# The FFN's second projection by tokens, in seven block products set between the slabs of the first projection

## The chip, the core and the metric

The kernel runs on one core of a Trainium2 chip. The metric is the device time of one launch in microseconds (us), taken over repeated runs. A core has five engines that run their own instruction streams and wait for one another by semaphores: TensorE (PE in the profile, with its weight loads as PEld), VectorE (DVE), ScalarE (ACT), GpSimd (POOL) and SyncE (SP), which here only issues DMA transfers. Matmul results land in PSUM, which has eight buffers of 128 x 512 float32 in this kernel (four in the pool mm, four in ms); everything else lies in SBUF.

## The reference

One step of a one-layer decoder: a mixer (a gated MLP and a state-space branch) and then the FFN that the change touches. There are 256 prompt tokens and 64 sample tokens (8 sequences of 8), D = 2048 and an inner width of 5632 in two halves, g and u.

```python
def conv_ffn(h, conv_state, w_up, conv_w, conv_b, w_down):
    up = h @ w_up
    up, new_conv = causal_depthwise_conv(up, conv_state, conv_w, conv_b)
    g, u = jnp.split(up, 2, axis=-1)
    return (jax.nn.gelu(g, approximate=True) * u) @ w_down, new_conv

def rms_norm(x, w):
    xf = x.astype(jnp.float32)
    y = xf * lax.rsqrt(jnp.mean(xf * xf, axis=-1, keepdims=True) + EPS)
    return (y * w.astype(jnp.float32)).astype(x.dtype)

f, new_ffn_conv = conv_ffn(rms_norm(x, p["norm_ffn_pre"]), ffn_conv_state, ...)
x = x + rms_norm(f, p["norm_ffn_post"])
```

All inputs and outputs are float32. `h @ w_up` is the first projection (2048 to 11264), `... @ w_down` the second (5632 to 2048).

## The kernel before, in words

**Precision.** A product of two float32 matrices is made of three matmuls on rounded parts: each operand is split into a high part (rounded to the type float32r, by ScalarE) and a low part (what is left, by VectorE), and high x high, low x high and high x low are added up (`accumulate`, L131; its three matmuls are lines L134 to L136). A matmul on plain float32 operands is recorded as two passes.

**Layout.** Activations are kept with features on partitions and the 320 tokens along the free axis. Weights are the stationary operand, 128 x 128, and tokens move, 320 columns.

**Slabs.** Weights come in slabs of 512 KB (`slab`, L109): SP loads the raw slab (tile wraw), ScalarE rounds it (whi, L123), VectorE takes the difference (wlo, L124). Each of the three tiles has three buffers. The block is marked with `tc.high_priority(offset=100000)`; `first()` (L103) is a stronger mark. The Tile planner fixes the order of each engine's queue when the kernel is built: it goes by these priorities and by its own costs, and an engine then takes its instructions strictly in that order.

**First projection.** `project` (L175) handles 512 output features, 4 PSUM buffers of the pool mm: 8 slabs of 512 KB, each with 24 matmuls, and after each slab it calls `tick()` (L157), which lets a background task from the list `bg` advance by one step (up to its next `yield`). In the FFN no background task is left. `ffn_up(g)` calls it twice (half 0: the columns of g, half 1: those of u) for the 512 features of chunk g; there are 11 chunks. `evac(half, j, ps)` takes one block of 128 features out of PSUM: VectorE scales it into tile pad (L1329, L1330), ScalarE and VectorE do the convolution (L1336, L1338), ScalarE the gelu; for half 1 VectorE multiplies the halves (L1347, L1348) and `split` makes the parts fhi and flo (L396, L397). GpSimd does small copies (L1326, L1327, L1340, L1341).

**Second projection.** `chunk_out(w, ck, hi, lo, ...)` (L234) multiplies one chunk's 4 x 128 features by 512 rows of w_down: 16 output blocks of 128, each 12 matmuls with 320 columns, after which the block is added to the tile acc_ffn (L247; chunk 0 copies it on ScalarE). The loop at L1409 first makes `ffn_up(g + 1)` and then `chunk_out` of chunk g, so that the gate of chunk g + 1 runs while PE works on chunk g. In the chunk before the last, VectorE turns x (tile x1_tok) into token order meanwhile (L1404).

**Last norm.** While the last chunk runs, each finished block is squared, scaled by the gain and turned to tokens in 32 x 32 blocks; then PE sums the squares over partitions (L1426, L1429), the root is taken on 10 columns (L1433 to L1438), and the scaled f and x are added by VectorE (L1474) and, for three of ten token groups, by ScalarE and PE (L1452, L1454, L1459). The output y is stored in a turned layout that the host puts right.

## Time and profile before

| what | value |
|---|---|
| time, median of 3 runs | 1748.42 us (1748.28 to 1748.61) |
| span of the profiled execution, first to last instruction | 1746.8 us |
| granted TensorE clock, mean over the span | 1.000 |
| one steady chunk (1000.5 to 1085.0 us): second projection of one, first projection of the next | 28.2 + 56.3 us |
| VectorE busy in these | 22.85 + 28.52 us |
| last matmul of the last chunk starts | 1732.62 us |

The page gives no other time of the profiled execution than its span; around the span the runs show 1.6 us more (1748.42 - 1746.8). In group lines the columns are line, engine, operation, out<-in, shape and count, and behind the bar busy us, mean ns of one, and the idle time ahead of it with what ended it. In the windows each engine has its busy time and its number of instructions.

### The profile page before, as it was taken

What the parts mean: (1) busy time and instruction counts of PE and PEld (TensorE: products, weight loads), DVE (VectorE), ACT (ScalarE), POOL (GpSimd) and SP (SyncE); (2) the same over time, 40 slices, a digit from 0 to 9 for tenths busy, and PEclk for the clock granted to TensorE, in tenths of its full rate; (3) what the DMA queues carried; (4) which work ended last, traced back from release to release, by engine and by line L of the source; (5) the groups of instructions that cost most, each with busy time, mean ns of one, the idle gap of its engine ahead of it and who ended that gap; (6) DMA issues with size and microseconds to landing.
All of it is one profiled execution on the core that took longest, in us unless ns stands there. A gap on an engine that the chain in (4) does not pass through costs nothing.

```text
span 1746.8 us, 31126 instructions
## 1 busy us (share of the span) xinstructions
PE 1738.5 (100%) x12063; PEld 1719.3 (98%) x12063; DVE 1178.0 (67%) x2009; ACT 819.4 (47%) x1198; POOL 323.5 (19%) x684
## 2 busy tenths in 40 slices
PE   9999999999999999999999999999999999999998
PEld 9999999999999999999999999999999999999997
DVE  6549863657879787778954566565756565657587
ACT  6344545334656664646544434343434343333336
POOL 2432230000423323121210101020201010101002
PEclk9999999999999999999999999999999999999999
DMA  8786655456676777665655554545544545454543
GB/s 257 230 231 183 183 176 154 151 163 192 214 221 208 218 225 210 211 187 155 195 154 151 151 154 149 150 155 147 159 145 151 155 149 152 152 153 151 148 158 109
DMA packets 228803, 303.85 MB, mean 174 GB/s; under 512 B 21680, under 2 KB 152624, under 8 KB 228464
## 3 DMA queue, kind: packets, MB, share of 16 engines
q1 hardware_dynamic: 211264, 272.68, 51.7%
q0 software_dynamic: 6176, 13.87, 2.7%
q10 hardware_dynamic: 11216, 15.31, 2.6%
q8 instruction: 95, 1.56, 0.4%
q14 instruction: 52, 0.43, 0.1%
HBM read 280.80 MB, written 19.69 MB: 172 GB/s over the span
## 4 chain that ended last, share of the span: by engine, by line
PE 99%; DMA 0%; ACT 0%; DVE 0%; SPq 0%; issue 0%; ACTq 0%
PE ps L134 21%; PE ps L135 20%; PE ps L136 20%; PE pd L134 10%; PE pd L135 10%; PE pd L136 10%; PE y_ps L1086 1%; PE ps_v L134 1%; PE ps_v L136 1%; PE ps_v L135 1%; PE yo_ps L1001 0%; PE up_ps L1018 0%; PE sg L808 0%; DMA wraw<-in_w_in 0%; PE fin_ps L1167 0%; PE xt_ps L412 0%
## 5 line engine op out<-in xcount | busy, mean ns | idle before, releaser
L124 DVE TENSOR_TENSOR wlo<-wraw,whi 128x1024 fp32r<-128x1024 f32 (+2 forms) x480 | 584.7, 1219 | 420.6 <-ACT whi L123 417.8
L123 ACT CAST whi<-wraw 128x1024 fp32r<-128x1024 f32 (+2 forms) x479 | 495.4, 1034 | 693.4 <-PE ps L135 392.3
L134 PE MATMUL ps<-h_hi,whi 128*128 128x320 f32 x2428 | 752.2, 310 | 0.0
L135 PE MATMUL ps<-h_lo,whi 128*128 128x320 f32 x2428 | 750.6, 309 | 0.0
L136 PE MATMUL ps<-h_hi,wlo 128*128 128x320 f32 x2428 | 750.0, 309 | 0.0
L134 PEld LDWEIGHTS ps<-h_hi,whi 128*128 128x128 f32 x2428 | 455.7, 188 | 3.1 <-issue 1.3
L135 PEld LDWEIGHTS ps<-h_lo,whi 128*128 128x128 f32 x2428 | 455.9, 188 | 0.4
L136 PEld LDWEIGHTS ps<-h_hi,wlo 128*128 128x128 f32 x2428 | 455.7, 188 | 0.0
L134 PE MATMUL pd<-fhi,whi 128*128 128x320 f32 x704 | 217.4, 309 | 0.0
L135 PE MATMUL pd<-flo,whi 128*128 128x320 f32 x704 | 217.4, 309 | 0.0
L136 PE MATMUL pd<-fhi,wlo 128*128 128x320 f32 x704 | 217.4, 309 | 0.0
L134 PE MATMUL pd<-ohi,whi 128*128 128x320 f32 x448 | 138.7, 310 | 0.0
L136 PE MATMUL pd<-ohi,wlo 128*128 128x320 f32 x448 | 138.3, 309 | 0.0
L135 PE MATMUL pd<-olo,whi 128*128 128x320 f32 x448 | 138.3, 309 | 0.0
L1341 POOL COPY ptf<-pad 128x2 f32<-128x2 f32 x88 | 22.0, 250 | 601.4 <-DVE pad L1329 600.8
L136 PEld LDWEIGHTS pd<-fhi,wlo 128*128 128x128 f32 x704 | 132.4, 188 | 0.0
L134 PEld LDWEIGHTS pd<-fhi,whi 128*128 128x128 f32 x704 | 132.3, 188 | 0.0
L135 PEld LDWEIGHTS pd<-flo,whi 128*128 128x128 f32 x704 | 132.3, 188 | 0.0
L247 DVE TENSOR_TENSOR acc_ffn<-acc_ffn,pd 128x320 f32<-128x320 f32 (+1 forms) x161 | 77.2, 480 | 29.8 <-PE pd L136 28.2
L134 PEld LDWEIGHTS pd<-ohi,whi 128*128 128x128 f32 x448 | 84.1, 188 | 0.6
L135 PEld LDWEIGHTS pd<-olo,whi 128*128 128x128 f32 x448 | 84.1, 188 | 0.3
L136 PEld LDWEIGHTS pd<-ohi,wlo 128*128 128x128 f32 x448 | 84.1, 188 | 0.0
(353 smaller groups left out, 1725.0 us busy)
## 6 DMA issues: line engine op xcount, KB each, us to landing
wraw<-in_ffn_w_up SPq DMA_DIRECT2D x176, 512.0 KB, 3.7
wraw<-in_w_in SPq DMA_DIRECT2D x132, 512.0 KB, 3.8
wraw<-in_ffn_w_down SPq DMA_DIRECT2D x88, 512.0 KB, 3.4
wraw<-in_w_out SPq DMA_DIRECT2D x64, 512.0 KB, 3.5
st<-in_state_ssm SPq DMA_DIRECT2D x40, 256.0 KB, 4.6
out_ssm_state_sample<-st ACTq DMA_DIRECT2D x30, 256.0 KB, 2.3
cs<-dacs_d SPq DMA_DIRECT2D x16, 320.0 KB, 5.3
wraw<-in_w_in SPq DMA_DIRECT2D x12, 384.0 KB, 3.8
```

The source lines that it names most:

```text
L123: rounded[:] = [act.copy(hi, raw).ins]
L124: lowered[:] = [dve.tensor_tensor(out=lo, in0=raw, in1=hi.bitcast(F32), op=ALU.subtract).ins]
L134: pe.matmul(ps, whi, xhi, start=first, stop=False)
L135: pe.matmul(ps, whi, xlo, start=False, stop=False)
L136: last_made[0] = pe.matmul(ps, wlo, xhi, start=False, stop=last).ins
L247: added_last[:] = [dve.tensor_tensor(out=acc[:, nb, ts], in0=acc[:, nb, ts], in1=ps[:, ts], op=ALU.add).ins]
L1086: pe.matmul(ps[64 * i:64 * i + 64, cols], w(hl), x(hl, m, cpx), tile_position=(0, 64 * i), **flags)
L1341: pool.tensor_copy(ptf[:, k, :], pad[:, 256:258])
```

## The change

The second projection is turned round: tokens become the stationary operand (128 at a time) and 512 columns of w_down move. The result has tokens on partitions.

For the 256 prompt tokens a chunk's product is cut into blocks: the activations into 2 x 2 (128 tokens by 256 features, names a11 to a22), and for each half m of the output columns (1024 of 2048) the weights into 2 x 2 (256 features by 512 columns, b11 to b22). Strassen's scheme in Winograd's form makes seven block products of these, with sums s1 to s4 on the activations' side and t1 to t4 on the weights' side. Each product is 6 matmuls. The seven products are summed over the chunks each for itself (tiles in_mix and in_fp); `together(m)` combines them once, at the end. The 64 sample tokens are multiplied in plain float32, two groups of 512 columns beside each other in the array by `tile_position`.

The second projection of chunk g - 1 is now a background task (`down_steps`) of `ffn_up(g)`: after each slab of the first projection one step, that is one product, is issued; the first two steps are empty and 14 follow. Chunks 0 to 9 go this way; the last has no first projection left beside it and is done in eight plain products (`down_plain`). The weight sums t1 to t4 are made by GpSimd, t2 to t4 in place in the loaded blocks. x is turned into token order after `ffn_up(0)` and written to DRAM (x1_rows), and read back at the end. The last norm works on rows of tokens, block by block (`one_block`, `whole`). The host turns the columns of w_down and the gain beforehand and the result afterwards.

```diff
-    def slab(src, half=0, begins=False):
+    def slab(src, half=0, begins=False, kept=None):
...
+            raw, hi, lo = (t[:, m * half:m * half + m] for t in (both[:1] + list(kept) if kept else both))
...
-            hi = fp.tile([P, 4, NT], F32R, tag="fhi", name="fhi", bufs=2)
-            lo = fp.tile([P, 4, NT], F32R, tag="flo", name="flo", bufs=2)
+            a = hp.tile([P, 4, NP], F32, tag="ohi", name="a")
+            a_s = fp.tile([P, 4, NS], F32, tag="a_s", name="a_s", bufs=2)
+            parts = Parts(a, a_s, g == NG - 1)
...
-                split(hi[:, j, :], lo[:, j, :], a)
+                parts.there(j)
...
+        class Parts:
...
+            def cut(self, name):
+                self.hi[name] = fp.tile([P, 2, P], F32R, name=f"{name}_hi")
+                self.lo[name] = fp.tile([P, 2, P], F32R, name=f"{name}_lo")
+                split(self.hi[name], self.lo[name], self.block(name))
+
+            def there(self, j):
...
+                if j == 1:
+                    self.cut("a11")
+                    if self.plain:
+                        self.cut("a21")
+                    else:
+                        combined("s3", "a11", ALU.subtract, "a21")
+                        self.cut("s3")
+                elif j == 3:
+                    self.cut("a12")
+                    self.cut("a22")
+                    if not self.plain:
+                        combined("s1", "a21", ALU.add, "a22")
+                        combined("s2", "s1", ALU.subtract, "a11")
+                        combined("s4", "a12", ALU.subtract, "s2")
+                        for name in ("s1", "s2", "s4"):
+                            self.cut(name)
+
         nxt = ffn_up(0)
-        for g in range(NG):
-            hi, lo = nxt
-            if g < NG - 1:
-                nxt = ffn_up(g + 1)
...
-            chunk_out(ffn_w_down, g, hi, lo, g == 0, done, apart=g == NG - 1)
+        for i in range(4):
+            st = hp.tile([P, SN, 4, 32], F32, tag=("ohi", "olo")[i % 2], name="in_turn")
+            dve.transpose(out=st, in_=x1[:, 4 * i:4 * i + 4].rearrange("p k (s f) -> p s k f", f=32))
+            for q in range(4):
+                e = 512 * q + P * i
+                pool.dma_start(x1_rows[:, e:e + P].rearrange("(s t) e -> t s e", t=32), st[32 * q:32 * q + 32].rearrange("p s k f -> p s (k f)"))
+
+        in_mix = hp.tile([P, 9, 512], F32, tag="acc_mix", name="in_mix")
...
+        def taken_in(to, ps, begins):
+            with first():
+                if begins:
+                    act.copy(to, ps)
+                else:
+                    dve.tensor_tensor(out=to, in0=to, in1=ps, op=ALU.add)
...
+        def sample_products(ps, a_s, k0, w, start, stop):
+            for k in range(2):
+                for h in range(2):
+                    last_made[0] = pe.matmul(ps[64 * h:64 * h + 64], a_s[:, k0 + k], w[h][:, 512 * k:512 * k + 512], start=start and k == 0,
+                                             stop=stop and k == 1, tile_position=(0, 64 * h)).ins
+
+        def down_steps(ck, parts):
+            def ready(raw):
+                with tc.high_priority(offset=100000):
+                    hi, lo = (wp.tile([P, 1024], F32R, tag=t, name=t, bufs=3) for t in ("whi", "wlo"))
+                    act.copy(hi, raw)
+                    dve.tensor_tensor(out=lo, in0=raw, in1=hi.bitcast(F32), op=ALU.subtract)
+                return hi, lo
+            yield
+            yield
+            for m in range(2):
...
+                def less(to, x, y):
+                    with tc.high_priority(offset=100000):
+                        pool.tensor_tensor(out=to, in0=raw[x], in1=raw[y], op=ALU.subtract)
...
+                for name in ("b11", "b12", "b22", "b21"):
+                    load(name)
+                product(1, "a11", "b11")
+                yield
+                raw["t1"] = fp.tile([P, 1024], F32, name="t1")
+                less(raw["t1"], "b12", "b11")
+                ps = misc("pms")
+                sample_products(ps, parts.a_s, 0, (raw["b11"], raw["b12"]), True, False)
+                sample_products(ps, parts.a_s, 2, (raw["b21"], raw["b22"]), False, True)
+                taken_in(f_s[m], ps, ck == 0)
+                product(2, "a12", "b21")
+                yield
+                raw["t3"] = raw["b12"]
+                less(raw["t3"], "b22", "b12")
+                product(5, "s1", "t1")
+                yield
+                raw["t2"] = raw["b11"]
+                less(raw["t2"], "b22", "t1")
+                product(7, "s3", "t3")
+                yield
+                raw["t4"] = raw["b21"]
+                less(raw["t4"], "t2", "b21")
+                product(3, "s4", "b22")
+                yield
+                product(6, "s2", "t2")
+                yield
+                product(4, "a22", "t4")
+                yield
...
+        for g in range(1, NG):
+            steps = down_steps(g - 1, nxt)
+            bg.append(steps)
+            nxt = ffn_up(g)
+            while bg:
+                advance(bg, steps)
+        for m in range(2):
+            together(m)
...
+        def one_block(c, nb):
+            t, g, _ = of(c, nb)
+            ends = c == 0 and nb == 3
+            with first() if ends else nullcontext():
+                act.activation(unread, t, AF.Square, accum_out=squares[:, c, nb:nb + 1])
+                (dve if ends else pool).tensor_tensor(out=t, in0=t, in1=g, op=ALU.mult)
+            if nb == (1 if c == 2 else 3):
+                whole(c)
...
+                for nb in range(2 if c == 2 else 4):
+                    t, _, y = of(c, nb)
+                    if nb == 2:
+                        act.activation(unread, t, AF.Copy, scale=r)
+                        pool.tensor_tensor(out=y, in0=unread, in1=y, op=ALU.add)
+                    else:
+                        dve.scalar_tensor_tensor(out=y, in0=t, scalar=r, in1=y, op0=ALU.mult, op1=ALU.add)
...
+        act.activation(fp.tile([P, 1], F32, name="root_ready"), eps, AF.Sqrt)
+        down_plain(NG - 1, nxt, one_block)
```

`down_plain` takes w_down in slabs as `chunk_out` did, multiplies each by the blocks of both token groups, 96 matmuls with 512 columns in all, and does the samples as above. In its second half the products of the first token group come last, from weights that are kept until then.

More of the change, by code (lines that the diff above doesn't have):

```diff
@@ L1382, in ffn_up @@
                 act.dma_start(o_fconv_s[:, k:k + 4], stg[:, half])
[L1383 to L1385 removed]
+            return parts
         eps = fp.tile([P, 1], F32, name="eps")
         pool.memset(eps, EPS)
[L1388 to L1400 removed]
@@ L1420, in hybrid_step @@
-        act.dma_start(o_fconv_p, ptf)
-        ps = misc("tsum")
-        with tc.issue_after(pd_last[-1]):
-            made = pe.matmul(ps[:, :NT], ones, sq4, start=True, stop=False).ins
-        for ts in parts_of(KD - 1):
-            with tc.issue_after(made):
-                made = pe.matmul(ps[:, ts], ones, one[0][:, ts], start=False, stop=ts.stop == NT).ins
-        sums = fp.tile([P, SN, 32], F32, name="sums")
-        dve.transpose(out=sums, in_=ps[:, :NT].rearrange("p (s f) -> p s f", f=32))
```

197 lines of the change are left out of this document (128 added, 69 removed).

## The prediction

> **What bounds the kernel now.** I read the page first (the span, busy shares, the chain that ended last, the groups), then the windows of one steady chunk of the FFN, then the chain in order of time for the cost of single products, then forms, waits and timelines.
>
> ```profile
> span 1746.8 us, 31126 instructions
> PE 1738.5 (100%) x12063; PEld 1719.3 (98%) x12063; DVE 1178.0 (67%) x2009; ACT 819.4 (47%) x1198; POOL 323.5 (19%) x684
> PE 99%; DMA 0%; ACT 0%; DVE 0%; SPq 0%; issue 0%; ACTq 0%
> ```
> ```profile
> 1000.50:1028.70 28.20, 28.20 (x195) 28.20 (x194) 22.85 (x43) 10.98 (x14) 3.58 (x10) 1.00 0.50 152
> 1028.70:1085.00 56.30, 56.30 (x386) 56.30 (x386) 28.52 (x42) 22.11 (x26) 6.69 (x23) 1.00 0.50 152
> ```
> ```profile
> 1000.49:1028.66 28.17, 28.17 (x192) 28.07 (x192) 7.26 (x15) 0.00 (x0) 1.00 0.49 152
> ```
>
> TensorE is the bound: 99% of the chain. In the windows (columns: PE, PEld, DVE, ACT, POOL, clock, DMA share, GB/s) the second projection of one chunk takes 28.2 us and the first 56.3 us, PE without a gap, at clock 1.00; the last row, of tile pd alone, counts the second projection's 192 products in 28.17 us, 0.147 each. VectorE works 22.85 + 28.52 = 51.4 us of those 84.5. A microsecond taken from PE comes off the time as long as PE's operands stay ahead.
>
> **The change part by part. PE.** A chunk's second projection is 192 products with 320 moving columns. For ten of the eleven chunks it becomes 2 halves x 7 products x 6 matmuls = 84 rounded products with 512 columns, and 2 x 8 sample products in full fp32 with 64 stationary columns, in pairs beside each other. Prices:
>
> ```profile
> 679.02 0.69 PE s_ps L991 x3
> 800.34 1.72 PE fin_ps L1167 x4
> 734.76 1.69 PE y_ps L1086 x32
> 736.45 0.34 PE ps L134
> 736.79 0.15 PE ps L135
> ```
> ```profile
> L1086 PE MATMUL y_ps<-cs,xdt 128*64 128x128 f32 x128 | 10.1, 279 | 0.0
> L1086 PE MATMUL y_ps<-cpx,s 128*64 128x128 f32 x64 | 6.2, 273 | 0.0
> L1086 PE MATMUL y_ps<-cs,xdt 128*64 128x64 f32 x64 | 4.5, 220 | 0.0
> ```
>
> s_ps are rounded products of 512 columns: 0.69 / 3 = 0.23 us each; 84 make 19.3. fin_ps are fp32 products of 512 columns, each recorded as two passes: 1.72 / 2 = 0.86. Whether two 64-column products share the array is shown by y_ps: its records (two for a product, in 8 visits of 32) hold (64 x 128 + 32 x 128 + 32 x 64) / 8 = 1792 columns a visit; one after the other at 0.86 per 512 that is 3.01 us, in pairs 1.51; the visit took 1.69. So pairs it is. A visit costs 0.18 over the pairs, and the next product 0.34 instead of 0.15: 0.35 for going in and out. A half's samples: 8 x 0.86 / 2 + 0.35 = 3.8 us (bounds: 3.4 with free switching, 7.2 unpaired). Chunk: 19.3 + 7.6 = 26.9 against 28.2, so **-12.5 us** over ten.
>
> The last chunk stays plain: 96 x 0.23 + 7.6 = 29.7, **+1.5 us**.
>
> **VectorE, GpSimd, ScalarE.** Per chunk the weights to lower rise from 24 to 30 (L124), 16 additions of 320 become 16 of 512, and four splits of 320 become seven cuts and four combinations of 256. In the rows the count stands behind x, then busy us, then the mean ns of one.
>
> ```profile
> L124 DVE TENSOR_TENSOR wlo<-wraw,whi 128x1024 fp32r<-128x1024 f32 x460 | 568.8, 1237 | 412.1 <-ACT whi L123 409.6
> L123 ACT CAST whi<-wraw 128x1024 fp32r<-128x1024 f32 x460 | 482.0, 1048 | 684.8 <-PE ps L135 392.3 <-PE pd L135 145.9 <-issue 97.8
> L247 DVE TENSOR_TENSOR acc_ffn<-acc_ffn,pd 128x320 f32<-128x320 f32 x159 | 76.7, 482 | 29.8 <-PE pd L136 28.2
> L397 DVE TENSOR_TENSOR flo<-a,fhi 128x320 fp32r<-128x320 f32 x44 | 21.4, 488 | 1.6 <-ACT fhi L396 1.1
> L1020 DVE TENSOR_TENSOR st<-st,up_ps 128x512 f32<-128x512 f32 x32 | 20.5, 682 | 4.9 <-PE up_ps L1018 4.9
> L1347 DVE TENSOR_TENSOR a<-ucv,gcv 128x256 f32<-128x256 f32 x44 | 18.4, 418 | 0.0
> ```
>
> VectorE: 51.4 + 6 x 1.24 - 16 x 0.48 + 16 x 0.68 - 4 x 0.49 + 11 x 0.42 = 64.7 us of the new chunk's 56.3 + 26.9 = 83.2, or 78%. ScalarE goes from 33.1 by 6 x 1.05 and a little for cuts to some 41: no bound. New on GpSimd are 8 subtractions of 1024 a chunk, and these take VectorE's time too:
>
> ```profile
> 436.69 0.73 POOL L1063 TENSOR_TENSOR cpx<-cpx,cT 128x256 f32<-128x256 f32 x1 [11.17 <-ACT cpx L1062]
> 1729.43 0.88 POOL L330 TENSOR_TENSOR sq<-sq,sq 128x320 f32<-128x320 f32 x1 [1.20 <-ACT sq L329]
> ```
> ```profile
> 437.75 4.08 POOL L1012 TENSOR_TENSOR st<-st,tote 128x512 f32<-128x512 f32 x3 [0.33 <-PE yo_ps L1001]
> 437.87 2.02 DVE L124 TENSOR_TENSOR wlo<-wraw,whi 128x1024 fp32r<-128x1024 f32 x1 [1.73 <-ACT whi L123]
> ```
>
> By (0.88 - 0.73) / 64 a column, 1024 columns take 0.88 + 704 x 0.0023 = 2.5 us, 20 us a chunk. A lowering that met a GpSimd operation took 2.02 instead of 1.24 and the three GpSimd operations stretched to 4.08: they take turns. If every subtraction held VectorE for its whole length the chunk would need 64.7 + 20 = 84.7 us of 83.2; evacuations from PSUM and idle time take part of it. [...]
>
> What does a full VectorE cost PE? Windows in which both were nearly full:
>
> ```profile
> 440.00:460.00 20.00, 20.00 (x139) 20.00 (x138) 19.30 (x36) 14.93 (x31) 12.49 (x19) 1.00 0.61 187
> 540.00:560.00 20.00, 20.00 (x156) 19.65 (x156) 20.00 (x38) 13.38 (x22) 7.50 (x16) 1.00 0.52 167
> ```
> ```profile
> ACT whi L123 <- PE ps L135: 186.2, 78, 2.5
> ```
>
> VectorE at 97 to 100% with GpSimd busy 7.5 to 12.5 us of 20, and PE lost nothing. But the lead shrinks: today ScalarE waits up to 2.5 us for PE to free one of three buffers; three slabs of 3.5 us are 10.5 us of work. With products (1.4 us) between slabs in the same buffers a buffer comes free 4.9 us before it is needed, and rounding and lowering take 1.05 + 1.24, so 2.6 us are left, about one subtraction. Bounds: nothing, or one missed lowering (1.2) a half, 24 us. The two windows are nearer: I take **+2.5 us** over ten chunks.
>
> **SP's queue.** Loads stay at 512 KB, 8 a chunk, but a half's four loads go into single buffers and are issued between slab loads. The load of b21 for the second half waits until t4, made in place in the old one, is lowered, and the next slab's load queues behind. That lowering needs the buffer which a slab frees; counting from there: 2.3 us to round and lower, some 3.7 to land (row below), 2.3 to round and lower that slab, 8.3 in all; PE wants it after two slabs and three products, 2 x 3.5 + 3 x 1.4 = 11.2. Covered, by 2.9 us; without the cover it is part of the stalls above.
>
> ```profile
> wraw<-in_ffn_w_up SPq DMA_DIRECT2D x176, 512.0 KB, 3.7
> 1089.26 0.42 DVE L1347 TENSOR_TENSOR a<-ucv,gcv 128x256 f32<-128x256 f32 x1
> 1094.75 0.42 DVE L1347 TENSOR_TENSOR a<-ucv,gcv 128x256 f32<-128x256 f32 x1
> 1098.58 0.42 DVE L1347 TENSOR_TENSOR a<-ucv,gcv 128x256 f32<-128x256 f32 x1
> 873.48 0.41 DVE L1347 TENSOR_TENSOR a<-ucv,gcv 128x256 f32<-128x256 f32 x1
> ```
>
> **Both ends of the stage.** Today the second projection of the chunk before covers the convolution and gate of the last columns. With the first projection ended at 1085.0, blocks 1, 2 and 3 were gated only at 1089.3, 1094.8 and 1098.6. In the last chunk PE now wants blocks 0 and 1, cut, 1.4 us after that end. If VectorE is as slow there: a wait to about 5.2, then two slabs and half the samples (7.4), then a wait to 14.6 for blocks 2 and 3: 3.8 + 2.0 = 5.8 us. With PE waiting, less competes on VectorE; bounds 0 and 8, I take **+3.0**. Behind it 4.1 MB of gains and x1 rows are loaded beside weights: 0 to 3, **+0.5**. At the start, x1 is turned (four transposes on VectorE) and written out before the room of acc_mix is free for the sums; chunk 0's last block was gated at 873.5 and PE wants it about 875. Four PSUM buffers hold products meanwhile, but ScalarE's first copies wait with the slab casts behind them, and PE for those: 0 to 10, **+1.0**. The 16 write-outs on POOL's queue hide beside the slabs; uncovered they are part of that 10.
>
> **The tail.**
>
> ```profile
> 1732.62 0.31 PE L136 MATMUL pd<-fhi,wlo 128*128 128x320 f32 x1
> 1735.19 0.31 ACT L1433 ACTIVATE last_s<-sums,eps 128x10 f32<-128x10 f32 x1 [1.27 <-DVE sums L1431]
> 1735.92 0.17 DVE L1437 SCALAR_TENSOR_TENSOR last_t<-last_s,last_r 128x10 f32<-128x10 f32 x1
> 1741.82 0.34 ACTq L1461 DMA_DIRECT2D out_y<-f_tok  x1
> L1474 DVE SCALAR_TENSOR_TENSOR f_tok<-f_tok,last_r,x_tok 128x512 f32<-128x512 f32 x6 | 4.1, 747 | 0.0
> L1452 ACT ACTIVATE f_tok<-f_tok,last_r 128x512 f32<-128x512 f32 x3 | 2.1, 716 | 1.2 <-DVE last_r L1438 0.8 <-ACT f_tok L1459 0.4
> ```
>
> Now 14.0 us run from the last product to the end, 5.0 of them after the last issue. After: addition 0.68, square 0.72, reduction and root 0.5, four small steps 0.9, three blends 2.2, GpSimd's blend in between 1.3, handovers 0.4, write 5.0: 11.7, so **-2.5** (-4 to 0, if the other tokens' norms queue ahead).
>
> Sum: -12.5 + 1.5 + 2.5 + 3.0 + 0.5 + 1.0 - 2.5 = -6.5. From the span, 1746.8, that is 1740.3; the median of the three runs, 1748.42, stands 1.6 above the span, so **1741.9 us**. About 0.2% (3.5 us) is what a measurement of this kernel can tell from no change.
>
> **The rivals.**
> - *Subtractions starve the lowering* (slower). The three subtractions after the samples come in a row, 7.5 us, with one VectorE operation between two; a lowering is missed per half. The 64.7 + 20 us against 83.2 speak for it, the two full windows against. 20 x 1.2 = 24 us instead of 2.5: 1763. With my other terms the gain is gone from 0.65 us of stall a chunk above mine. [...]
> - *Everything is hidden.* No stalls, no exposed ends: -12.5 + 1.5 - 2.5 = -13.5: 1735. The full windows speak for it; the gating rows against.
> - *The ends show in full.* 5.8 us in the last chunk, 8 at the start, 1 for loads, for my 4.5: 1752. For it: nothing of the old cover is left. Against: VectorE is free while PE waits.
> - *The pairs don't run beside each other at 512 columns*, so the change doesn't do what it says: 3.4 us more a half, 22 halves, +76: 1818. The y_ps visits speak against it.
>
> **How the numbers follow.** Forecast 0.45 (0.37 faster, 0.08 same), all hidden 0.20 (faster), ends 0.14 (half same, half slower), starved 0.19 (0.18 slower, 0.01 same), unpaired 0.02 (slower): faster 0.57, same 0.16, slower 0.27. The range runs from just under all hidden to the starved case, 1734 to 1763; the likeliest case's own is 1737 to 1747.
>
> **What would show it.** In a window of a steady chunk: 83.2 to 83.6 us instead of 84.5, sample visits of about 3.8 us, products 0.23 apart, VectorE above 80%. Waits of PE for whi or wlo, and lowerings of 2 to 4 us beside GpSimd's subtractions, would show the starved case; waits of PE for the cuts (names ending in _hi, _lo) near the last chunk's start, the ends. The last product should lie 11 to 12 us before the end. The prediction is wrong if the planner's order of VectorE leaves too little lead with 2.6 us for 4.7.

## The result, and the profile after

The changed kernel takes 1790.41 us (median of four runs, 1787.64 to 1792.64), the kernel before beside it 1748.35 us (1748.10 to 1748.61). The ratio is 1.0241, with a 95% interval from 1.0226 to 1.0255: 42.1 us slower, where 6.5 us faster was forecast. The profiled execution took 1788.48 us, 1.7 us more than its span. On the page of the changed kernel the lines that answer to those of before are:

```profile
span 1786.8 us, 29669 instructions
...
PE 1743.2 (98%) x11223; PEld 1610.1 (90%) x11223; DVE 1358.1 (76%) x2128; ACT 882.1 (49%) x1274; POOL 601.9 (34%) x789
...
PE 43%; DVE 3%; issue 1%; DMA 1%; ACT 1%; POOL 0%; DVEq 0%; ACTq 0%
```

TensorE has 840 instructions fewer and is busy longer, and waits now stand in the chain. Where they lie is seen when the span is cut by stage: the first chunk (from the end of `ffn_up(0)` to the start of `ffn_up(2)`), eight steady chunks, the plain last chunk (from the last of the seven-product tasks to the last product) and the tail. The windows of the changed kernel (columns: PE, PEld, DVE, ACT, POOL, clock, DMA share, GB/s):

```profile
859.23:964.97 105.74, 90.75 (x502) 77.08 (x501) 73.38 (x101) 52.90 (x75) 48.22 (x75) 0.95 0.47 143
964.97:1636.62 671.65, 670.14 (x4002) 592.97 (x4001) 544.81 (x773) 321.40 (x394) 289.08 (x318) 1.00 0.50 152
1721.50:1768.00 46.50, 39.31 (x129) 22.03 (x128) 25.58 (x47) 16.01 (x29) 12.65 (x13) 0.89 0.46 150
1768.00:1786.80 18.80, 0.52 (x3) 0.30 (x2) 10.76 (x22) 3.41 (x10) 5.85 (x4) 0.63 0.42 139
```

And the last chunk and the tail of the kernel before:

```profile
1704.60:1732.80 28.20, 28.20 (x194) 28.07 (x192) 22.34 (x41) 21.45 (x38) 12.09 (x12) 1.00 0.23 75
1732.80:1746.80 14.00, 7.36 (x19) 2.91 (x18) 8.04 (x20) 4.78 (x10) 0.00 (x0) 0.94 0.51 187
```

| stage | before | after | difference | forecast |
|---|---|---|---|---|
| up to the end of `ffn_up(0)` | 859.7 | 859.2 | -0.5 | 0 |
| first chunk | 84.5 | 105.7 | +21.2 | 0 (-1.0 and the start's +1.0) |
| eight steady chunks | 8 x 84.49 | 671.65 = 8 x 83.96 | -4.3 | -8.0 |
| tenth chunk | 84.5 | 84.9 | +0.4 | -1.0 |
| plain last chunk | 28.2 | 46.5 | +18.3 | +5.0 |
| tail | 14.0 | 18.8 | +4.8 | -2.5 |
| sum | | | +40.0 | -6.5 |

In the middle the change does what it was said to do, at half the size. In the chain the two kinds of visits have the forecast lengths, 1.4 us (6 x 0.23) for a product and 3.6 us (forecast 3.8) for half the samples, so that the pairs do run beside each other:

```profile
1661.43 1.40 PE pm L1455 x6
...
1691.26 3.58 PE pms L1461 x16
```

The loss is at the two ends: 21.2 + 18.3 + 4.8 = 44.3 us. The clock column says that more was lost there than the length of the waits: behind some of them TensorE ran at half its clock, a product of 512 columns every 0.43 us instead of 0.23, and in the third window below one of 320 every 0.27 instead of 0.15. The windows lie inside three such stretches of the changed kernel. The trace's clock records have the first from 1725.1 to 1731.9 (6.8 us), the other two at 3.4 us each:

```profile
1728.80:1731.50 2.70, 2.70 (x7) 2.16 (x7) 2.70 (x7) 0.41 (x1) 0.00 (x0) 0.50 1.01 231
1742.10:1745.40 3.30, 3.30 (x9) 2.59 (x9) 1.13 (x2) 2.26 (x5) 2.24 (x2) 0.51 0.02 5
872.00:875.00 3.00, 3.00 (x13) 3.00 (x12) 2.99 (x4) 1.83 (x2) 1.56 (x4) 0.50 0.01 1
```

### The profile page after: what moved, and what is told of

Its sections match the earlier page's. It is cut to its first block, busy times and chain, and to the rows that moved or that the text cites. A ratio compares the mean times of both kernels' runs of the same rounds, so it can differ in the third digit from the quotient of the medians.

```text
span 1786.8 us, 29669 instructions
## 1 busy us (share of the span) xinstructions
PE 1743.2 (98%) x11223; PEld 1610.1 (90%) x11223; DVE 1358.1 (76%) x2128; ACT 882.1 (49%) x1274; POOL 601.9 (34%) x789
## 5 line engine op out<-in xcount | busy, mean ns | idle before, releaser
L124 DVE TENSOR_TENSOR wlo<-wraw,whi 128x1024 fp32r<-128x1024 f32 (+2 forms) x399 | 513.8, 1288 | 178.2 <-ACT whi L123 176.9
L123 ACT CAST whi<-wraw 128x1024 fp32r<-128x1024 f32 (+2 forms) x398 | 411.3, 1034 | 413.1 <-PE ps L135 136.1
L1470 DVE TENSOR_TENSOR wlo<-b,whi 128x1024 fp32r<-128x1024 f32 x120 | 174.1, 1451 | 85.1 <-ACT whi L1469 85.1
L1469 ACT CAST whi<-b 128x1024 fp32r<-128x1024 f32 x120 | 125.7, 1047 | 172.6 <-PE ps L135 135.5
L1486 POOL TENSOR_TENSOR b<-b,b 128x1024 f32<-128x1024 f32 x40 | 115.1, 2896 | 1.4 <-PE pms L1461 1.4
L1343 POOL COPY ptf<-pad 128x2 f32<-128x2 f32 x88 | 38.5, 438 | 222.1 <-DVE pad L1331 220.0
L1486 POOL TENSOR_TENSOR b<-b,t 128x1024 f32<-128x1024 f32 x20 | 67.4, 3372 | 101.1 <-PE pms L1461 92.9
L134 PEld LDWEIGHTS pd<-ohi,whi 128*128 128x128 f32 x448 | 84.1, 188 | 0.6
L135 PEld LDWEIGHTS pd<-olo,whi 128*128 128x128 f32 x448 | 84.1, 188 | 0.3
L136 PEld LDWEIGHTS pd<-ohi,wlo 128*128 128x128 f32 x448 | 84.1, 188 | 0.0
L1461 PE MATMUL pms<-b,a_s 128*64 128x512 f32 x320 | 74.4, 599 | 2.8 <-DVE a_s L1349 2.8
L247 DVE TENSOR_TENSOR acc_mix<-acc_mix,pd 128x320 f32<-128x320 f32 (+1 forms) x113 | 54.1, 481 | 28.2 <-PE pd L136 28.0
L1455 PE MATMUL pm<-whi,s_hi 128*128 128x512 f32 x160 | 64.1, 401 | 5.9 <-ACT in_mix L1448 5.9
```

Of the source, the lines that this page charges most:

```text
L123: rounded[:] = [act.copy(hi, raw).ins]
L124: lowered[:] = [dve.tensor_tensor(out=lo, in0=raw, in1=hi.bitcast(F32), op=ALU.subtract).ins]
L134: pe.matmul(ps, whi, xhi, start=first, stop=False)
L135: pe.matmul(ps, whi, xlo, start=False, stop=False)
L136: last_made[0] = pe.matmul(ps, wlo, xhi, start=False, stop=last).ins
L247: added_last[:] = [dve.tensor_tensor(out=acc[:, nb, ts], in0=acc[:, nb, ts], in1=ps[:, ts], op=ALU.add).ins]
```

## The experiments

All are edits to the changed kernel. Times are medians, the other columns come from each run's one profiled execution. Executions of kernels that leave a stage alone scatter: the first chunk took 102.3 to 105.7 us in five of them, the last chunk 46.5 to 50.1, a steady chunk 83.9 to 84.2 (with GpSimd's subtractions) or 83.4 to 83.7 (without). Smaller differences are not read. The windows shown are cut within 0.3 us of the stages of the table. The runs that hold products back behind the last first projection (e4, e14, e17, e20) are not in the table, since their last chunk is cut elsewhere.

| run | time | first chunk | steady chunk | last chunk | tail |
|---|---|---|---|---|---|
| before | 1748.4 | 84.5 | 84.5 | 28.2 | 14.0 |
| changed kernel | 1790.4 | 105.7 | 84.0 | 46.5 | 18.8 |
| e1, states' loads first | 1781.2 | 97.9 | 83.9 | 46.6 | 18.7 |
| e2, sums' room later | 1782.1 | 91.6 | 84.0 | 49.1 | 18.8 |
| e3, e1 and e2 | 1778.0 | 91.8 | 84.0 | 46.5 | 18.7 |
| e5, subtractions on VectorE | 1784.1 | 103.1 | 83.5 | 47.0 | 19.2 |
| e6, e3 and e5 | 1766.6 | 84.5 | 83.6 | 50.1 | 19.2 |
| e7, subtractions of 64 columns | 1778.4 | 99.6 | 83.4 | 49.6 | 18.7 |
| e8, gains and x1 behind three slabs | 1785.8 | 105.3 | 84.0 | 41.0 | 18.2 |
| e9, own room for three slabs | 1776.3 | 102.3 | 84.1 | 39.0 | 15.1 |
| e12, tail alone | 1789.2 | 104.2 | 84.2 | 49.7 | 15.2 |
| e10, e6, e9 and e12 | 1748.8 | 84.3 | 83.6 | 38.2 | 11.1 |
| e13, e10 and gating first | 1754.2 | 85.6 | 83.7 | 43.8 | 11.5 |
| e15, e13 and e8 | 1746.9 | 83.8 | 83.6 | 33.4 | 14.6 |
| e16, e10 and e8 | 1746.2 | 84.4 | 83.6 | 37.0 | 10.8 |
| e19, e15 and the whole tail on VectorE | 1746.9 | 84.8 | 83.6 | 33.6 | 13.9 |

### The start: what stands ahead in a queue

The first suspect is two loads of 32 KB. The convolution needs the states fst. SP's queue of the changed kernel (start, length, what) has them behind the four loads of b, which are marked with a high priority:

```profile
845.88 0.37 SPq L1482 DMA_DIRECT2D b<-in_ffn_w_down  x1
...
847.32 0.97 SPq L1482 DMA_DIRECT2D b<-in_ffn_w_down  x2
...
850.99 0.47 SPq L1482 DMA_DIRECT2D b<-in_ffn_w_down  x1
...
855.04 2.54 SPq L1316 DMA_DIRECT2D fst<-in_fconv  x3
```

SP's queue and then GpSimd's of the kernel before:

```profile
846.07 1.29 SPq L1315 DMA_DIRECT2D fst<-in_fconv  x3
```
```profile
848.82 0.74 POOL L1327 COPY pad<-fst 128x16 f32<-128x16 f32 x5 [2.44 <-DMA fst<-in_fconv]
```

GpSimd's queue of the changed kernel: the copies from fst stand behind the first weight subtraction, t1, which itself waits for b; ScalarE's convolution waits for the copies (last line, from the waits):

```profile
860.79 2.40 POOL L1486 TENSOR_TENSOR t<-b,b 128x1024 f32<-128x1024 f32 x1 [7.66 <-DMA b<-in_ffn_w_down]
863.13 0.74 POOL L1329 COPY pad<-fst 128x16 f32<-128x16 f32 x5
```
```profile
ACT gcv L1338 <- POOL pad L1329: 6.5, 1, 6.5
```

So the copies run at 863.1 instead of 848.8. The second suspect is the room for the sums: the tile in_mix lies where x1 lay, and ScalarE's first copy into it waits until x1 has been turned: the last of the four transposes starts at 913.7 and takes 1.5 us, and the copy starts at 915.3. (The last write-out goes out only at 921.0, so that not all of the writing is waited for.) TensorE's waits in the first chunk:

```profile
PE pm L1455 <- ACT in_mix L1448: 5.9, 1, 5.9
PE pms L1461 <- DVE a_s L1349: 2.8, 1, 2.8
PE ps L136 <- DVE wlo L124: 2.3, 4, 0.9
PE ps L134 <- DVE pad L1332: 2.2, 1, 2.2
```

e1 puts the loads of fst first (64 KB by the page's rows, 22 loads of 32.0 KB, two a chunk; the text below says 80); the planner then also sets t1 behind the copies.

```diff
-                sp.dma_start(fst[:, half], fconv[:, k:k + 4])
+                with first() if g == 0 else nullcontext():
+                    sp.dma_start(fst[:, half], fconv[:, k:k + 4])
```

> Edit: the two loads of the convolution states of chunk 0 (fst, 80 KB) go ahead of the four loads of b blocks on SP's queue, as they stood in the kernel before; nothing else. Theory (queue order): in the changed kernel these loads are issued at 855.0 to 859.8 instead of 846.1, the pad copies run at 863.1 instead of 848.8, and the gating of chunk 0 is 6 to 10 us late; the first chunk (105.7 us for 84.0 steady) should shrink by 6 to 11 us, and the run by as much: 1779 to 1784. Rival (the room of acc_mix alone): the copies into in_mix at 915.3 set the length, whatever happens before; the run moves by less than 2 us: 1788 to 1792.

1781.23 us, first chunk 97.9: the queue order is a cause, 4 to 8 us of it. e2 lets the first half's sums go into in_fp, which is free, so that in_mix is needed half a chunk later.

```diff
-        in_fp = fp.tile([P, 7, 512], F32, name="in_fp")
-        sums_of_m = [[t[:, i] for i in range(7)] for t in (in_mix, in_fp)]
-        f_s = [in_mix[:, 7 + m] for m in range(2)]
+        in_fp = fp.tile([P, 8, 512], F32, name="in_fp")
+        sums_of_m = [[t[:, i] for i in range(7)] for t in (in_fp, in_mix)]
+        f_s = [t[:, 7] for t in (in_fp, in_mix)]
```

> Edit: the sums of half 0 go into in_fp and those of half 1 into in_mix, so that the room of acc_mix is first written half a chunk later; f_s lies half in either. Theory: PE stood some 10 us between 895 and 916 for ScalarE's copies into in_mix, which waited for x1 to be turned and written out; this goes: first chunk 105.7 to about 95, run 1779 to 1783. Rival (the turning delays PE by its own work, transposes on VectorE and write-outs, wherever the sums lie): under 3 us: 1787 to 1791.

1782.05 us, 8.4 less, as the theory had it; the first chunk fell to 91.6, more than expected, and the wait for in_mix is gone. Waits for the late gating, 2.8 us for a_s and 1.5 for pad, are left.

> Edit: the two edits above together. If they are separate losses the gains add: 16 to 20 us, run 1770 to 1774, first chunk 86 to 90. If the one hides the other (a late gating makes the in_turn rooms late, and so the room of acc_mix) the two together give little more than the larger one: 1777 to 1782.

1778.0 us (1774.9 to 1781.3), first chunk 91.8: the two do not add. In e3 the two waits for the gating that e2 still had are gone, and one of 4.1 us for a slab's lowering stands in the first chunk instead; that the late gating had only hidden it is argued. 7.8 us over a steady chunk remain. Most of them are this wait and a lowered clock behind it (0.83 in the mean from 890 to 900, which is 1.7 us), and the queues of VectorE and GpSimd show its cause. TensorE's longest wait in e3:

```profile
PE ps L136 <- DVE wlo L124: 4.7, 2, 4.1
```

VectorE, and then GpSimd, in e3 just before it:

```profile
879.44 0.41 DVE L1414 TENSOR_TENSOR s<-a,s 128x256 f32<-128x256 f32 x1
879.77 3.39 DVE L1471 TENSOR_TENSOR wlo<-t,whi 128x1024 fp32r<-128x1024 f32 x1
883.09 5.16 DVE L398 TENSOR_TENSOR s_lo<-s,s_hi 128x256 fp32r<-128x256 f32 x2
```
```profile
879.72 2.37 POOL L1487 TENSOR_TENSOR b<-b,t 128x1024 f32<-128x1024 f32 x1 [1.91 <-PE pms L1462]
882.05 5.92 POOL L1487 TENSOR_TENSOR b<-b,b 128x1024 f32<-128x1024 f32 x2
```

While GpSimd makes three subtractions in a row, VectorE gets three operations done in 8.5 us (3.39 + 5.16), worth 2.0 us: two cuts of 256 columns took 5.16 us instead of 0.75. In these rows the engines take turns instruction by instruction. A slab's lowering, at 891.0, stands behind the cuts and behind two transposes of x that follow them (2.9 us). e5 and e6 move the subtractions to VectorE, alone and on top of e3; e7 leaves them on GpSimd but makes them narrow: it leaves out 960 of 1024 columns of each difference, and t1 becomes one tile that is filled with zeros beforehand.

```diff
-                        pool.tensor_tensor(out=to, in0=raw[x], in1=raw[y], op=ALU.subtract)
+                        dve.tensor_tensor(out=to, in0=raw[x], in1=raw[y], op=ALU.subtract)
```
```diff
-                        pool.tensor_tensor(out=to, in0=raw[x], in1=raw[y], op=ALU.subtract)
+                        pool.tensor_tensor(out=to[:, :64], in0=raw[x][:, :64], in1=raw[y][:, :64], op=ALU.subtract)
```

> Edit: the eight subtractions of weights in a chunk are made by VectorE instead of GpSimd; nothing else. Theory (three subtractions in a row hold VectorE): while they run, 8.3 us, VectorE gets three operations done, 2.0 to 2.5 us of work, in every half; a steady chunk has room for that, the first and the last don't, because the gating stands behind. On VectorE the three take 3 x 1.2 = 3.7 us. First chunk 105.7 to 100 to 103, the part from the last first projection on 46.5 to 41 to 44, steady chunks 84.0 within 0.5; run 1780 to 1786. Rival (VectorE is simply full): 8 x 1.24 = 9.9 us more work a chunk on VectorE makes the steady chunks longer, by 0.5 to 2 us each: 1795 to 1810.

> Edit: the states' loads first, the sums' room later (both as before) and the subtractions on VectorE. With the first two edits alone the run was 1778, the first chunk 91.8 us, and its longest wait of PE, 4.1 us, was for a lowering that stood behind two cuts which took 5.16 us for 0.75 beside the subtractions. Theory (row of subtractions): that wait goes, the first chunk comes to 85 to 88, the run to 1766 to 1773. Rival (VectorE is full at the start whoever subtracts): first chunk 91 to 93, the run 1776 to 1785.

> Edit: each subtraction on GpSimd covers 64 columns instead of 1024 (the four differences of a half are then not made, the rest of the work stands); this prices all that GpSimd's subtractions cost. Theory: steady chunks fall from 83.96 to 83.0 to 83.4 (56.3 for the first projection and 26.9 for the second, without a stall), the first chunk to 100 to 103, the last part to 41 to 44: run 1774 to 1782. Rival (the subtractions are hidden everywhere, ends are gating and loads alone): steady 83.8 to 84.0, run 1787 to 1791.

e6 took 1766.61 us, as the theory of the row had it, and its first chunk has no wait of TensorE above 0.6 us left; the windows of the first chunk in e3 and in e6:

```profile
859.55:951.39 91.84, 85.71 (x502) 75.52 (x501) 73.05 (x92) 47.05 (x67) 45.61 (x62) 0.98 0.54 164
```
```profile
860.45:944.91 84.46, 83.83 (x502) 74.19 (x501) 70.06 (x99) 48.68 (x67) 22.60 (x52) 1.00 0.57 173
```

So three causes make up the first chunk's loss, and with all three gone it is within a microsecond of a steady chunk. The eight steady chunks in e5 and in e7:

```profile
963.17:1631.09 667.92, 667.92 (x4002) 593.10 (x4000) 570.15 (x837) 318.02 (x395) 81.68 (x255) 1.00 0.50 153
```
```profile
960.17:1627.58 667.41, 667.41 (x4001) 593.30 (x4000) 502.21 (x773) 317.68 (x392) 125.69 (x321) 1.00 0.50 153
```

Without the subtractions a steady chunk takes 667.41 / 8 = 83.43 us with TensorE never idle: that is its own time. GpSimd's subtractions add 0.53 us to it (83.96), VectorE's 0.06 (83.49), which lies inside the scatter, although VectorE is then 85% busy. e5 took 1784.05 us and e7 1778.43, as expected; but both were expected to shorten the last chunk to 41 to 44 us, and it stayed at 47.0 and 49.6. The last chunk's loss is another one.

### The last chunk: who holds the room of a slab

Of the last chunk's 18.3 us the forecast had 1.5 for the plain products, 3 for the gating and 0.5 for loads. The first part is dearer even without a wait, because the samples are not done in two visits: the program multiplies them after every second slab, and the planner scatters them further between the prompt products. Two of these visits of the changed kernel, of four products (two records each) and of a single one:

```profile
1746.60 1.94 PE L1461 MATMUL pds<-wraw,a_s 128*64 128x512 f32 x8
1750.05 1.07 PE L1461 MATMUL pds<-wraw,a_s 128*64 128x512 f32 x2
```

A single product has no partner in the array and pays for going in and out besides: it took 1.07 us, 0.86 of them by the price of fin_ps; the four took 0.49 each. e15 below, whose last chunk has no wait of TensorE, has seven such visits and an eighth just ahead of it, and takes 33.4 us where 29.7 were forecast. The rest are waits and the halved clock. TensorE's wait for a_s, ScalarE's longest wait, and the waits of SP's queue in the same stretch of the changed kernel:

```profile
PE pds L1461 <- DVE a_s L1349: 3.9, 2, 2.8
```
```profile
ACT whi L123 <- DMA wraw<-in_ffn_w_down: 10.1, 3, 6.8
```
```profile
SPq L117 <- PE pds L1461: 36.8, 4, 14.1
```

SP's queue waited in the last stretch of the kernel before too (24.8 us for acc_ffn), and TensorE lost nothing there, so the line alone is no price. e4 tests the first line: the last seven-product task starts four slabs later, so that four products stand behind the last first projection and cover its gating.

```diff
-            yield
-            yield
+            for _ in range(6 if ck == NG - 2 else 2):
+                yield
```

> Edit: in the last chunk but one the products start four slabs later, so that four of its 14 products stand behind the end of the last first projection, and cover the gating of the last chunk. Theory (exposed gating): of the last chunk's 46.5 us (30 without a wait) about 4 to 6 are waits for a_s and the cuts right after the first projection; they go: 1784 to 1787. Rival (late weights and a halved clock are the loss, the gating lies beside them): 1788 to 1792.

1787.85 us, between the two. The wait for a_s went, and one of 4.0 us for the lowering of a held product's weights came, behind GpSimd's subtractions, which by then stood beside the gating. From the start of the tenth chunk to the last product e4 took 130.3 us, the changed kernel 131.2: the wait was moved. e8 and e9 test the other two lines. In e8 the loads of gains stand behind the third slab and those of the x1 rows behind the sixth (not the fourth, as the text below has it) in SP's queue, instead of going out from GpSimd's queue at the chunk's start.

```diff
-        pool.dma_start(gain, norm_last[0:1, :].broadcast_to([P, D]))
...
+                            if (m, i, nb) == (0, 1, 0):
+                                gains_in()
+                            if (m, i, nb) == (1, 0, 3):
+                                x1_in()
```

> Edit: the loads of gains and x1 rows (4.1 MB) go on SP's queue behind the third and fourth slab of the last chunk, instead of GpSimd's queue at the end of the last first projection. Theory (contention): ScalarE's cast waited 6.8 us for a slab that landed at 1738.2, and cuts queued behind it cost PE 1.7 us, a later slab 1.5 us: 2 to 5 us go, run 1785 to 1788. Rival (the slab is late for another reason, the gating sets the time): within 1.5 us, 1789 to 1792.

1785.83 us, within the theory's range, last chunk 41.0. e9 goes to SP's line. The samples are multiplied in plain float32, so they read wraw itself; the room of a slab is free only after its sample products, and the next load waits for them. Three of the five later slabs get rooms that have fallen free elsewhere:

```diff
+                        own = {(0, 1, 1): "b22", (1, 0, 2): "t1", (1, 0, 3): "b21"}.get((m, i, nb))
-                        wb = slab(rows_of(ffn_w_down, 4 * ck + 2 * i, 2, 512 * nb, 512), kept=kept)
+                        wb = slab(rows_of(ffn_w_down, 4 * ck + 2 * i, 2, 512 * nb, 512), kept=kept,
+                                  own=own and fp.tile([P, 1024], F32, tag=own, name="own"))
```

> Edit to the changed kernel: in the last chunk the fourth, fifth and sixth slab land in the rooms of b22, t1 and b21, which are free by then, instead of in wraw; nothing else. Theory (the samples hold wraw): sample products read the weights in full fp32, so that wraw is not free once lowered, as it was before, but only after the sample products; SP's loads wait 36.8 us for these in the last chunk, and slabs four to eight come late. Last part 46.5 to 39 to 43, run 1783 to 1787. Rival (only the gating sets the time): the slabs come early and PE waits as long: within 1.5 us, 1789 to 1792.

1776.30 us: 14 us from this edit alone, the largest of all, and more than either theory gave. SP's waits for sample products in the last chunk of e9, and the chunk's window:

```profile
SPq L119 <- PE pds L1463: 15.6, 2, 9.5
```
```profile
1718.56:1757.80 39.24, 34.26 (x131) 20.30 (x130) 29.52 (x50) 17.48 (x34) 16.35 (x15) 0.96 0.55 165
```

The last chunk falls to 39.0 us, the granted clock there rises from 0.89 to 0.96, and TensorE waits only for a_s (2.8 us) and 0.5 us beside. The tail too became 3.7 us shorter, though nothing of it was touched. VectorE is busy for 7.7 us in it, in the changed kernel for 10.8; that this makes the difference is argued, not shown. The rest of the 14 us, some 3, lies in the first chunk's scatter.

### The tail

In the changed kernel VectorE's queue in the tail reads (three lines of it):

```profile
1768.68 1.75 DVE L1635 SCALAR_TENSOR_TENSOR x_tok<-in_fp,last_r,x_tok 128x512 f32<-128x512 f32 x1
...
1770.36 0.68 DVE L1450 TENSOR_TENSOR in_fp<-in_fp,pd 128x512 f32<-128x512 f32 x1
...
1776.88 1.41 DVE L1635 SCALAR_TENSOR_TENSOR x_tok<-in_mix,last_r,x_tok 128x512 f32<-128x512 f32 x2
```

The last product is done at 1768.0, but its addition starts at 1770.4, behind the blends of the other prompt block (the last of them 1.75 us beside a GpSimd addition); then the sample tokens' norm goes through the same queue, and the last block's blends start only at 1776.9. e12 puts the samples' squares ahead and lets VectorE blend all of the last block.

```diff
-            with first() if ends else nullcontext():
+            with first() if ends or c == 2 else nullcontext():
...
-                    if nb == 2:
+                    if nb == 2 and c == 1:
```

> Edit to the changed kernel: in the tail the sample tokens' squares and multiplications by the gains go ahead of other work, and the last prompt block's third quarter is blended by VectorE; nothing else. Theory (order in the tail): from the last product to the end 18.8 to 12 to 14.5 us, run 1784 to 1787. Rival (the tail is long because the slabs before it were late, as it fell to 15.1 with own rooms for these alone): 17.5 to 19, run 1788 to 1792.

The tail fell to 15.2 us, nearer to the theory's 12 to 14.5 than to the rival's 17.5 to 19, but the run took 1789.23 us (1782.66 to 1791.99): the trace speaks for the theory, the time cannot tell it from no change. With everything together:

> Edit: the three edits of the 1766.6 us run, own rooms for the three slabs, and in the tail the sample tokens' squares and the multiplications by the gains ahead of other work, and the last prompt block's third quarter blended by VectorE. Theory: last part 48.7 to 40 to 43, and from the last product to the end 19.4 to 12 to 15, as the sample tokens' norm then lies ahead of the last block: 1752 to 1758. Rival (the tail's length is VectorE's own work): tail 18 to 19, 1758 to 1762.

1748.82 us, ratio to the kernel before 1.0002 (0.9992 to 1.0011), and the last chunk and tail of e10 read:

```profile
1696.71:1735.10 38.39, 34.15 (x131) 20.26 (x130) 29.37 (x55) 17.47 (x34) 17.13 (x16) 0.96 0.54 171
1735.10:1746.00 10.90, 0.00 (x0) 0.00 (x0) 6.48 (x15) 1.01 (x3) 0.94 (x1) 0.61 0.46 144
```

Six small edits to order and rooms, none to the arithmetic but the engine of the subtractions, give back the whole 42 us.

### Is there a faster version?

What is left in e10's last chunk is a wait of 2.8 us for a_s with a lowered clock behind it (0.66 in the mean from 1700 to 1705). e13 gives the convolution and gate of the last chunk's second half a higher mark than its weights; e14 holds two products back besides.

```diff
+            def evac(half, j, ps):
+                with tc.high_priority(offset=150000) if g == NG - 1 and half else nullcontext():
+                    taken(half, j, ps)
```

> Edit: as the run with room and tail, and in the last chunk the convolution and gate of the second half go ahead of the lowering of the last chunk's weights. Theory (exposed gating): the waits for a_s (3.3) and the cuts shrink by 2 to 5 us: 2 to 5 us below the run with room and tail. Rival (VectorE is then late with the weights): within 1 us or longer.

> Edit: as the run with gating first, and the products of the last chunk but one two slabs later, so that two or more stand behind the last first projection and cover its gating. Theory: 1 to 3 us below the run with gating first. Rival (what is moved behind is only moved): within 1 us.

1754.19 and 1756.18 us, both slower than e10 and than their theories. The wait for a_s went; in e14 one of 6.2 us for a slab's load came in its place, and in e13 this one:

```profile
PE pd L1462 <- ACT whi L125: 3.1, 1, 3.1
```

Whether gains and x1 rows delayed the slab is told by moving them, with the gating first (e15) and without (e16); e17 holds two products back in e10.

> Edit: as the run with gating first (1754.2), and the loads of gains and x1 rows on SP's queue behind the third slab and later. Theory (these loads delayed the slabs there, ScalarE's cast waited 3.1 us): 3 to 7 us below that run: 1747 to 1751. Rival (the gating first delays the lowering of weights itself): 1753 to 1756.

> Edit: as the run with room and tail (1748.8), and the loads of gains and x1 rows on SP's queue behind the third slab and later. In that run no slab came late, the wait was for the gating: theory: within 1.5 us, 1747.3 to 1750.3. Rival (the loads slow slabs even where no wait shows): 1744 to 1747.

> Edit: as the run with room and tail (1748.8), and the products of the last chunk but one two slabs later, so that two more stand behind the last first projection. Theory (exposed gating): the 3.0 us wait for a_s goes, with the 1.7 us of lowered clock behind it: 1744 to 1747. Rival (only moved: VectorE lowers the held products' weights ahead of the gating): 1748 to 1751.

e15 took 1746.86 us, 7.3 less than e13: the loads did it. In its last chunk TensorE never waits (window of e15):

```profile
1696.99:1730.55 33.56, 33.56 (x127) 19.70 (x126) 29.23 (x44) 14.80 (x27) 11.30 (x8) 1.00 0.50 167
```

But the tail is 14.6 us for e10's 11.1: most of what TensorE gained is given back there, where VectorE still has 9.7 us to do, in e10 6.5. e16 took 1746.15 us (ratio 0.9990, 0.9981 to 1.0000), as the rival had it, but not shown for its reason: its waits for a_s are 3.5 us in all, and its last chunk is 1.2 us shorter than e10's with the clock at 1.00 throughout. e17 took 1747.51 (0.9997, 0.9987 to 1.0006), above its theory. Its wait for a_s was still 3.5 us: moved again. The last two go for e15's tail, with every block blended by VectorE, and with two products held.

```diff
-                    if nb == 2 and c == 1:
-                        act.activation(unread, t, AF.Copy, scale=r)
-                        pool.tensor_tensor(out=y, in0=unread, in1=y, op=ALU.add)
-                    else:
-                        dve.scalar_tensor_tensor(out=y, in0=t, scalar=r, in1=y, op0=ALU.mult, op1=ALU.add)
+                    dve.scalar_tensor_tensor(out=y, in0=t, scalar=r, in1=y, op0=ALU.mult, op1=ALU.add)
```

> Edit: as the run with gating and loads (1746.9), and every quarter of the prompt blocks is blended by VectorE, so that GpSimd's addition no longer stretches a blend to 1.75 us and ScalarE's room for squares is not held by it. Theory: tail 14.5 to 11 to 12.5, run 1743.5 to 1745.5. Rival (the sample tokens' norm still lies ahead of the last block): tail 13.5 to 14.5, run 1746 to 1748.

> Edit: as the run with the tail on VectorE, and the products of the last chunk but one two slabs later. No wait of TensorE for the gating was left without it, so theory: within 1.5 us of that run. Rival (the samples' scattered visits, 0.2 to 0.4 us each, fall together): 1 to 3 us below it.

1746.94 us (0.9992, 0.9983 to 1.0001) and 1747.09 (0.9995, 0.9986 to 1.0004); the tail of e19 stayed at 13.9, as its rival had it. So the best versions stand 1.2 to 2.3 us below the kernel before, at the edge of what can be measured. In e16 ten chunks gain 0.1 + 8 x 0.9 + 0.8 = 8.1 us and the tail 3.2, and the last chunk takes 8.8 us more: what the scheme saves on TensorE is spent on the one chunk that it does not fit.

## Why the prediction was wrong

**PE, -12.5: right but for 0.2 us a chunk.** The prices came out: 1.40 us a product, 3.58 us half the samples, and a steady chunk without the subtractions takes 83.4 us where 83.2 were forecast. (The working's own figures, 28.2 and 26.9, give 13.0 over ten chunks and not 12.5.)

**The plain last chunk, +1.5: mis-sized.** It has the samples at 7.6 us, in two visits and all in pairs. In e15, with no wait and the clock at 1.00, the chunk takes 33.4 us, which is +5.2: the samples come in seven visits and one ahead, some of a single product.

**VectorE, GpSimd, +2.5: the mechanism right, the size twice that.** 83.96 - 83.43 = 0.53 us a chunk, 5.3 over ten, between the two ends given (0 and 24). Two evacuations from PSUM lost nothing beside a subtraction: in the changed kernel they took 0.68 and 0.69 us within one that ran from 1067.26 to 1071.63, and one took 0.68 at 1064.40 with none. The rival "Subtractions starve the lowering" named the three subtractions in a row, and e3's rows show just that; in a steady chunk the lead swallows most of it. But the term was spread evenly over ten chunks, and the stall falls where the lead is gone: some 7 us in the first chunk (e3 to e6).

**SP's queue, "covered by 2.9 us": the step that failed.** It was worked out for a steady chunk, and there it holds. It counted what the loads of b do to slabs and not what they do to the small loads beside them: the states at the start (e1, 4 to 8 us). And for the plain last chunk it has no reckoning of a slab's room at all. There the samples read the raw slab, so that a load waits for sample products, and the first of these for the gating: 36.8 us of SP's waits. With own rooms for three slabs the last chunk came from 46.5 to 39.0 (e9). GpSimd's queue was named for the 16 write-outs alone; that t1 would sit at its head waiting for b, ahead of the copies that the convolution needs, was not looked for.

**Both ends, +3.0, +0.5 and +1.0.** The gating wait of the last chunk was there: 3.9 us for a_s and 1.7 for two cuts of the second half (0.9 and 0.8), 5.6 in all. That is near the 5.8 that had been worked out; the 3.0 taken in its place was too little, and the halved clock behind the waits was in no term. The loads of gains and x1 rows, +0.5 with 0 to 3 as bounds, cost about 5 us in the chunk (46.5 to 41.0 in e8). At the start the wait for in_mix was named ("ScalarE's first copies wait with the slab casts behind them, and PE for those: 0 to 10"), and taken at 1.0 for no row that was nearer to 0 than to 10; e2 takes 11 to 14 us off the first chunk and 8.4 off the run. It is the turning of x1 that holds the copies, not the writing out of all of it. The rival "The ends show in full" was the right one in kind, and at 1752 far too short, since it had the gating and the room but neither the states nor the samples' hold on the slabs.

**The tail, -2.5.** The working of 11.7 us was right for a tail in which the last block is first in every queue: e10 has 11.1. (That the two lie so close is partly luck, since e10 has no GpSimd blend in the last block and the working had one at 1.3 us.) In the changed kernel the other prompt block and the sample tokens queue ahead, which the bound (0 at worst) did not reach: 18.8.

**The range.** It ended at the dearest single rival. The upper bounds of all terms together (24 + 8 + 3 + 10 + 0, with -12.5 and +1.5) make +34, some 1782 us, and even that falls short of 1790: the states, the samples' hold on the slabs, their scattered visits, the halved clock and a longer tail stood in no bound.

## What to carry to other kernels

Where work is moved from a stage of its own into the shadow of another, price the first and the last pass by themselves, with the queues written out instruction by instruction: what hid the ends before is what has been moved away. For every new reader of a buffer ask when the buffer now comes free and which load waits for that; for every new instruction with a high mark ask what small thing it now stands ahead of. And a wait that is taken from the end of a chain has to be followed to the last instruction: here e4, e13, e14 and e17 only moved it.

## What the runs showed of the hardware that was not expected

Behind short waits of TensorE more was lost than their own length. In the changed kernel a wait of 2.2 us for pad ended at 870.6, and from 871.75 to 875.16 the granted clock was 0.50. Two waits of 0.9 and 0.8 us for cuts ended at 1739.6 and 1740.9, and from 1742.15 to 1745.56 it was 0.50 again, with 0.43 us for a product instead of 0.23. It was not so behind every wait: behind one of 2.9 us for a_s e16 stayed at 1.00, where e10, behind one of 2.8, had 0.66 in the mean from 1700 to 1705. Beside the row of GpSimd subtractions in e3, 2.4 to 3.0 us each, VectorE got one operation done for each of them: a lowering of 1024 columns in 3.39 us, and two cuts of 256 columns in 2.6 each, 0.38 us of work. And the time of the changed kernel scatters by 5 us between executions (1787.64 to 1792.64), that of the kernel before by 0.5 in the four beside it and by 2.5 in 25. The scatter goes down to 4.0 us in e10 and 2.3 in e15, as the waits at the ends are removed. In the changed kernel the longer executions have the lower mean clock (0.988 at 1792.64, 0.991 at 1787.64, and 0.003 of 1790 us are 5.4 us); in e8 they have not (0.991 at 1788.10, 0.990 at 1782.37). So the halved clock can be a part of the scatter, and what sets it off is not known.
